# Norm sums as columns that share a PSUM bank, half of proj_a's sums accumulated in DRAM, and modulation spread wider, in a one-core decoder layer

## The chip, the cores and the metric

The kernel runs on one core of one Trainium2 chip. Its time is the device time of one execution in microseconds (us). The engines are TensorE (PE; PEld is its weight load), VectorE (DVE), ScalarE (ACT), GpSimd (POOL) and SyncE (SP), the last of which here only issues DMAs. POOL issues DMAs too, among them the ones that accumulate into DRAM, and ACT issues a few.

## The reference

One decoder layer on 1024 tokens of width 1024 in float32, followed by a final RMS norm. The parts that matter here:

```
u = modulate(rms_norm(x, norm1_g), sh1, sc1)
x = x + 0.5 * g1 * swiglu(u, ffn1_w_up, ffn1_w_down)
u = modulate(rms_norm(x, norm2_g), sh2, sc2)
z = u @ w_in + b_in
...
m = sigmoid(mg_a) * (ya @ proj_a) + sigmoid(mg_b) * (yb @ proj_b)
x = x + g2 * (m @ w_out)
u = modulate(rms_norm(x, norm3_g), sh3, sc3)
x = x + 0.5 * g3 * swiglu(u, ffn2_w_up, ffn2_w_down)
return rms_norm(x, final_g)
```

The nine shifts, scales and gates (sh1 to g3) come from one product of silu(c) with a 1024 x 9216 matrix (`mod_w`). `ya` is the output of a gated linear recurrence, `yb` that of an S5 state-space part.

## The kernel before

Data lie transposed: the 128 partitions hold features, the free dimension holds tokens. The 1024 features are eight tiles d = 0 to 7, and the tokens two halves h of 512. Float32 products are made from rounded parts: an operand is split into hi (rounded to fp32r by ACT) and lo (the rest, a subtraction on DVE), and a product is three passes, hi x hi, hi x lo and lo x hi. Many products are made in pairs by seven block products for what would be eight, with sums and differences of the operands and of the results on DVE (`pair`, `pair_operands`).

Nothing is issued as it is written. `Plan` records each instruction (line 437 issues them all, so most rows of the trace name that line) and `order` (line 257) simulates the engines with the costs of `cost` (line 205), and takes on each engine the earliest-written instruction that is ready and has buffers; `ahead` moves the rank of some forward. The result is a fixed order per engine, in which each engine later waits in turn. So a changed cost or a changed place in the text can move instructions far away.

Side work is spread through the products: `spread` (line 465) takes a job and a rate, and each block product calls `tick`, which lets the job go on by that rate. In the first feed-forward block, `background` (line 1723) runs `s5_setup` at rate 1.0 and 24 `modulations` at `MOD_RATE`; 24 more run later at `LATE_RATE`. A modulation (line 681) is a 512 KB weight load, one 128x1024 multiply with a running sum on DVE, and two one-column instructions. `finish_jobs` (line 478) puts what is left of the jobs into the program in one go.

An RMS norm needs the sum of x squared over features, which lie on partitions. `norm` (line 1670), at the start, squares on ACT and multiplies by a 128x128 matrix of ones in full float32 (two recorded passes per product), so that the bank holds the sum in all 128 rows of 512 columns. `square` and `rstd` (lines 704, 717), for the later norms, first add the squares on DVE, split the total into hi and lo, and make two fp32r products with the ones. Both then call `rstd_of` (line 729): a square root on ACT and a reciprocal on DVE over 128x512. ACT loads a table when it changes its function. `modulate` (line 738) multiplies x by the result, applies scale and shift on ACT, and splits hi and lo. The last norm, in `on_out` (line 1749), runs in pieces of 512, 256 and 256 tokens; its products with `final_g` run on DVE or, for tiles named in `OUT_POOL`, on POOL, each followed by its output DMA.

In `Mixer.run` (line 1495) `q_d` in DRAM holds the gated `proj_b` products. Four pairs of `proj_a` tiles follow. For each of their 16 results (tile d, half h), DVE multiplies the result by the gate loaded from `mga_d`, and adds what it loads from `q_d`. For the first two pairs (`M_OUT = 2`) the sum t is stored to `m_d` and loaded again, to free its buffer; for the last two it stays. Then each m is split into hi and lo, and the `w_out` products begin.

Of the kernel before, what the change touches and what calls it, by code (L numbers as in the profile page):

```python
# [10 lines left out]
F32 = mybir.dt.float32  # L11
# [34 lines left out]

SETUP_RATE, MOD_RATE, GAIN_RATE, LATE_RATE = 1.0, 0.18, 0.1, 0.2

# [25 lines left out]
class Plan:  # L74
# [130 lines left out]
    def cost(self, call, table):  # L205
# [236 lines left out]
class Layer:  # L442
# [260 lines left out]

    def square(self, st, x, d):

        nc = self.nc
        n = x.shape[1]
        sq = self.act()[:, :n]
        nc.scalar.activation(sq, x, AF.Square)
        if st[0] is None:  # L710
            st[0] = sq
        else:
            acc = self.act()[:, :n]
            nc.two(ALU.add, acc, st[0], sq)
            st[0] = acc

    def rstd(self, st):

        nc = self.nc
        n = st[0].shape[1]  # L720
        hi, lo = self.tmp(F32R)[:, :n], self.tmp(F32R)[:, :n]
        nc.scalar.activation(hi, st[0], AF.Copy)
        nc.vector.tensor_sub(lo, st[0], hi.bitcast(F32))
        ps = self.bank()[:, :n]
        self.mm(ps, self.ones, hi, True, False)
        self.mm(ps, self.ones, lo, False, True)
        return self.rstd_of(ps)

    def rstd_of(self, ps):
        nc = self.nc  # L730
        n = ps.shape[1]
        root = self.tmp()[:, :n]
        nc.scalar.activation(root, ps, AF.Sqrt, bias=self.eps, scale=1.0 / D)
        r = self.act()[:, :n]
        nc.vector.reciprocal(r, root)
        return r

    def modulate(self, x, r, l, d):

        nc = self.nc  # L740
        if r is not None:
            nc.two(ALU.mult, x, x, r)
# [274 lines left out]
def s5_setup(L):  # L1017
# [4 lines left out]
    L.decay = L.con("decay", [P, 16])  # L1022
    L.ident = L.con("ident", [P, P])
    st = {}

    def params():
        softplus_scales(L)
        yield
        make_identity(L.tc.nc, L.ident)
        bc = [L.act(), L.act()]  # L1030
# [216 lines left out]
class Mixer:  # L1247
# [247 lines left out]
    def run(self):  # L1495
# [54 lines left out]
        for p, pair in enumerate(PROJ_A):  # L1550
            c11, c12, c21, c22 = L.pair(L.pair_weights([io["proj_a"][d] for d in pair]), ya)
            for e, h, c in ((0, 0, c11), (1, 1, c22), (1, 0, c21), (0, 1, c12)):
                d = pair[e]
                t, r = self.load(self.mga_d, d, h), self.load(self.q_d, d, h)
                nc.vector.tensor_mul(t, t, c)
                nc.two(ALU.add, t, t, r)
                if p < M_OUT:
                    nc.sync.dma_start(self.m_d[d][:, h * H : (h + 1) * H], t)
                    with nc.ahead(GATED_AHEAD):
                        m[h][d] = self.load(self.m_d, d, h)  # L1560
                else:
                    m[h][d] = t
        ms = [[None] * 8, [None] * 8]
# [3 lines left out]
        x = [[None] * 8, [None] * 8]  # L1567
        st = [[None], [None]]
        u3 = L.u3 = [[], []]

        def put(d, h, ps):
# [3 lines left out]
            nc.sync.dma_start(L.x2_d[d][:, h * H : (h + 1) * H], t)  # L1575
            L.square(st[h], t, d)
            x[h][d] = self.load(L.x2_d, d, h) if d < W_PAIRED else t
            if d == ND - 1:
                s = L.rstd(st[h])
                for e in range(ND):  # L1580
# [40 lines left out]
def hybrid_layer(ctx: ExitStack, tc: tile.TileContext, io):  # L1621
# [5 lines left out]
    L.gsc = L.con("gsc", [P, 24])  # L1627
    L.ones = L.con("ones", [P, P], F32R)
    L.eps = L.con("eps", [P, 1])
    L.cact = L.con("cact", [P, D])  # L1630
    nc.vector.memset(L.eps, EPS)
    nc.vector.memset(L.ones.bitcast(F32), 1.0)

# [36 lines left out]
    def norm(h):  # L1670
        ps = L.bank()
        for d in range(ND):
            sq = L.act()
            nc.scalar.activation(sq, x[h][d], AF.Square)
            L.mm(ps, L.ones.bitcast(F32), sq, d == 0, d == ND - 1)
        r = L.rstd_of(ps)
        for d in range(ND):
            nc.two(ALU.mult, x[h][d], x[h][d], r)

# [46 lines left out]

    st = [[None], [None]]
    u2 = [[], []]

    def on_x(d, h, x):  # L1730
        L.square(st[h], x[h][d], d)
        if d == ND - 1:
            r = L.rstd(st[h])
            for e in range(ND):
# [11 lines left out]
    pieces = [(0, slice(0, H))] + [(1, slice(i * H // LAST, (i + 1) * H // LAST)) for i in range(LAST)]  # L1746
    st3 = [[None] for _ in pieces]

    def on_out(d, p, x):
        h, c = pieces[p]  # L1750
        L.square(st3[p], x[h][d][:, c], d)
        if d == ND - 1:
            scaled = {}
            for e in OUT_POOL[p]:
                scaled[e] = L.act()[:, : c.stop - c.start]
                nc.scalar.activation(scaled[e], x[h][e][:, c], AF.Copy, scale=L.col("final_g", e))
            r = L.rstd(st3[p])
            for e in range(ND):
                if e in scaled:
                    o = scaled[e]  # L1760
                    nc.gpsimd.tensor_mul(o, o, r)
                else:
# [108 lines left out]
```

## Time and profile before

| | us |
|---|---|
| median of 3 runs (2054.18 to 2054.97) | 2054.34 |
| the profiled execution | 2057.46 |
| its span in the trace | 2055.7 |
| PE busy in it | 1991.2 |
| DVE busy | 1554.1 |
| ACT busy | 1065.2 |
| POOL busy | 324.3 |

The mean granted TensorE clock is 0.987 of full speed. The profiled execution is 3.1 us above the median, and 1.8 us of its time lie outside the span. PE is busy for 97% of the span, so the whole rest is some 64 us: what matters is where those lie, and what PE waited for there.

### The profile page before, as it was taken

To read this page: it belongs to the slowest core of one execution; us is meant where nothing else is said; L and a number is where in the kernel's file an instruction comes from. 1 tells how busy PE (TensorE), PEld (TensorE's weight loads), DVE (VectorE), ACT (ScalarE), POOL (GpSimd) and SP (SyncE) were. 2 spreads that over 40 slices of the span, in tenths; PEclk is the share of its full clock that TensorE was granted. 3 is DMA by queue.
4 is the path that set the end of the run, shared out by engine and by line. 5 is a ranking of instruction groups with operands and counts; after the bars stand their busy time and mean duration, and the time that the engine had idled before them with its cause. 6 is when DMAs were issued, how large, how long until landed. Compare 5 with 4: busy or idle time off the path is not lost. (4 is left out here: it accounts for less than half of the span.)

```text
span 2055.7 us, 27034 instructions
## 1 busy us (share of the span) xinstructions
PE 1991.2 (97%) x8866; PEld 1635.7 (80%) x8866; DVE 1554.1 (76%) x3064; ACT 1065.2 (52%) x1842; POOL 324.3 (16%) x409
## 2 busy tenths in 40 slices
PE   6999999998999999999999999899999999999997
PEld 3888888886888878788878888677888888887886
DVE  8997777778969787767999597879544444497757
ACT  5744344344434574455789643447443344366753
POOL 0222122121011001100000011100111121134442
PEclk9999999999999999999999999999999999999998
DMA  7767676778756367787555689662765565589993
GB/s 261 192 156 208 180 197 185 198 193 265 238 156 178 130 172 206 217 251 248 174 173 196 230 253 280 210 235 74 173 159 133 129 150 136 123 210 220 203 230 127
DMA packets 188045, 393.06 MB, mean 191 GB/s; under 512 B 20992, under 2 KB 44672, under 8 KB 187904
## 3 DMA queue, kind: packets, MB, share of 16 engines
q1 hardware_dynamic: 121504, 278.45, 40.8%
q0 software_dynamic: 49536, 84.96, 24.6%
q10 hardware_dynamic: 16864, 27.93, 3.7%
q8 instruction: 69, 1.13, 0.2%
q14 instruction: 72, 0.59, 0.1%
HBM read 262.81 MB, written 92.27 MB: 173 GB/s over the span
## 5 line engine op out<-in xcount | busy, mean ns | idle before, releaser
L437 PE MATMUL ps_in<-act_in,wh_in 128*128 128x512 f32 (+1 forms) x5592 | 1685.6, 390 | 37.3 <-ACT act_in L437 12.5
L437 PEld LDWEIGHTS ps_in<-act_in,wh_in 128*128 128x128 f32 x5592 | 1050.0, 189 | 263.5 <-DVE act_in L437 17.2
L437 PE MATMUL ps_in<-act_in,wl_in 128*128 128x512 f32 (+1 forms) x2796 | 1047.7, 389 | 0.0
L437 ACT ACTIVATE wh_in<-wr_in 128x512 fp32r<-128x512 f32 (+2 forms) x544 | 323.8, 601 | 571.6 <-PE ps_in L437 451.7
L437 PEld LDWEIGHTS ps_in<-act_in,wl_in 128*128 128x128 f32 x2796 | 528.6, 189 | 107.6
L437 DVE TENSOR_TENSOR wl_in<-wr_in,wh_in 128x512 fp32r<-128x512 f32 (+2 forms) x544 | 352.3, 653 | 174.3 <-ACT wh_in L437 173.1
L437 DVE TENSOR_TENSOR act_in<-act_in,act_in 128x512 f32<-128x512 f32 (+3 forms) x632 | 400.0, 677 | 30.9 <-ACT act_in L437 24.0
L437 DVE TENSOR_TENSOR tmp_in<-ps_in,tmp_in 128x512 f32<-128x512 f32 x296 | 203.9, 689 | 160.3 <-PE ps_in L437 157.0
L437 ACT ACTIVATE act_in<-act_in 128x512 fp32r<-128x512 f32 (+3 forms) x414 | 238.0, 612 | 129.6 <-DVE act_in L437 107.0
L437 POOL DMA_DIRECT2D wr_in<-wr_in x148 | 136.5, 922 | 544.9 <-ACT wr_in L437 169.8
L437 ACT ACTIVATE tmp_in<-ps_in 128x512 f32<-128x512 f32 x130 | 76.3, 589 | 51.9 <-PE ps_in L437 44.2
L437 POOL DMA_DIRECT2D re_in<-in_ffn_w_up x40 | 35.6, 890 | 426.0 <-ACT re_in L437 307.0
L437 ACT ACTIVATE wr_in<-wr_in 128x512 f32<-128x512 f32 (+1 forms) x148 | 85.2, 594 | 23.3 <-DVE wl_in L437 21.9
L437 DVE TENSOR_TENSOR tmp_in<-tmp_in,ps_in 128x512 f32<-128x512 f32 x82 | 56.0, 685 | 41.7 <-PE ps_in L437 41.1
L437 ACT ACTIVATE wh_in<-re_in 128x512 fp32r<-128x512 f32 (+1 forms) x74 | 44.3, 599 | 67.9 <-PE ps_in L437 65.2
L437 DVE SCALAR_TENSOR_TENSOR mw_in<-mw_in,cact 128x1024 f32<-128x1024 f32 x56 | 68.3, 1220 | 8.3 <-DMA mw_in<-in_mod_w 8.2
L437 DVE TENSOR_TENSOR tmp_in<-tmp_in,tmp_in 128x512 f32<-128x512 f32 (+1 forms) x96 | 66.0, 688 | 5.8 <-ACT tmp_in L437 5.2
L437 DVE SCALAR_TENSOR_TENSOR act_in<-ps_in,mods,act_in 128x512 f32<-128x512 f32 (+1 forms) x68 | 46.2, 686 | 29.1 <-PE ps_in L437 28.9
L437 PE MATMUL ps_in<-act_in,act_in 128*128 128x256 f32 (+1 forms) x336 | 57.8, 317 | 3.8 <-DVE act_in L437 2.3
L437 PEld LDWEIGHTS ps_in<-act_in,act_in 128*128 128x128 f32 x336 | 49.2, 190 | 12.5 <-DVE act_in L437 4.9
L437 POOL DMA_DIRECT2D x_d<-tmp_in x48 | 50.2, 1266 | 53.0 <-ACT tmp_in L437 51.5
L437 ACT ACT_TABLE_LOAD x42 | 53.9, 1283 | 2.4 <-PEq L1860 1.7
(109 smaller groups left out, 1019.4 us busy)
## 6 DMA issues: line engine op xcount, KB each, us to landing
wr_in<-in_ffn_w_up SPq DMA_DIRECT2D x84, 512.0 KB, 3.7
mw_in<-in_mod_w SPq DMA_DIRECT2D x56, 512.0 KB, 4.3
wr_in<-wr_in POOLq DMA_DIRECT2D x108, 256.0 KB, 5.1
g_d<-tmp_in SPq DMA_DIRECT2D x88, 256.0 KB, 4.0
act_in<-g_d SPq DMA_DIRECT2D x88, 256.0 KB, 6.0
wr_in<-in_ffn_w_down SPq DMA_DIRECT2D x48, 384.0 KB, 4.0
wr_in<-in_w_in SPq DMA_DIRECT2D x36, 512.0 KB, 3.9
x_d<-tmp_in POOLq DMA_DIRECT2D x48, 256.0 KB, 7.5
```

What stands on the lines that cost most here:

```text
L437: getattr(getattr(self.nc, engine), method)(*map(self.place, args), **{k: self.place(v) for k, v in kwargs.items()})
```

## The change

Five things change.

1. `norm` copies the bank of sums to SBUF, and for each block of 128 tokens multiplies it by two columns of the identity, which puts the sums of 128 tokens into the rows of two columns: eight columns for 512 tokens. The square root and the reciprocal run on those (`rstd`), and one float32 product per block with the identity spreads the result back over 128 partitions, into a PSUM bank from which the multiplications read it.
2. The last norm does so too, without the copy: `square` splits the sum of the first seven squares and multiplies each block by two columns of ones; the four blocks share one bank, and only the first product opens it. The last square is added by a float32 product per block. POOL cannot read PSUM, so its tiles get a copy made by ACT.
3. The two norms between (`rstd_rows`) keep their form, but every norm now also takes a two-column square root right after its first square.
4. `proj_a`'s first two pairs no longer load `q_d`, add and store `m_d`: POOL adds t to `q_d` by an accumulating DMA, and SP loads `q_d` afterwards.
5. `MOD_RATE` falls from 0.18 to 0.14 and `LATE_RATE` from 0.2 to 0.16; `cost` gives small products on PE a higher floor.

```diff
-SETUP_RATE, MOD_RATE, GAIN_RATE, LATE_RATE = 1.0, 0.18, 0.1, 0.2
+SETUP_RATE, MOD_RATE, GAIN_RATE, LATE_RATE = 1.0, 0.14, 0.1, 0.16
...
-            return max(60.0, n * 1.7 if rhs.dtype == F32 else (n + 32) / 2.4), table
+            if rhs.dtype == F32:
+                return max(60.0 if method == "transpose" else 224.0, n * 1.7), table
+            return max(112.0 if n == 2 else 60.0, (n + 32) / 2.4), table
...
-    def square(self, st, x, d):
+    def square(self, st, x, d, rows=False):
         nc = self.nc
         n = x.shape[1]
         sq = self.act()[:, :n]
         nc.scalar.activation(sq, x, AF.Square)
-        if st[0] is None:
-            st[0] = sq
-        else:
+        if d == 0:
+            st[:] = [sq, None]
+            self.root(self.con(self.name("early"), [P, 2]), sq[:, :2])
+            return
+        if rows or d < ND - 1:
             acc = self.act()[:, :n]
             nc.two(ALU.add, acc, st[0], sq)
             st[0] = acc
-    def rstd(self, st):
+        if rows:
+            return
+        if d == ND - 2:
+            hi, lo = self.tmp(F32R)[:, :n], self.tmp(F32R)[:, :n]
+            nc.scalar.activation(hi, acc, AF.Copy)
+            nc.vector.tensor_sub(lo, acc, hi.bitcast(F32))
+            st[1] = self.bank()
+            for b in range(n // P):
+                c = slice(b * P, (b + 1) * P)
+                out = st[1][:, 2 * b : 2 * b + 2]
+                self.mm(out, hi[:, c], self.ones, b == 0, False, b > 0)
+                self.mm(out, lo[:, c], self.ones, False, True, b > 0)
+        if d == ND - 1:
+            for b in range(n // P):
+                self.mm(
+                    st[1][:, 2 * b : 2 * b + 2], sq[:, b * P : (b + 1) * P],
+                    self.ones.bitcast(F32), False, True, True,
+                )
+
+    def root(self, out, sums):
+        self.nc.scalar.activation(out, sums, AF.Sqrt, bias=self.eps, scale=1.0 / D)
...
+    def rstd(self, ps, n):
         nc = self.nc
+        k = n // P
+        r = self.con(self.name("rstd"), [P, 2 * k])
+        self.root(r, ps[:, : 2 * k])
+        nc.vector.reciprocal(r, r)
+        out = self.bank()[:, :n]
+        for b in range(k):
+            self.mm(
+                out[:, b * P : (b + 1) * P], r[:, 2 * b : 2 * b + 1].to_broadcast([P, P]),
+                self.ident, True, True,
+            )
+        return out
...
-                t, r = self.load(self.mga_d, d, h), self.load(self.q_d, d, h)
+                t = self.load(self.mga_d, d, h)
                 nc.vector.tensor_mul(t, t, c)
-                nc.two(ALU.add, t, t, r)
                 if p < M_OUT:
-                    nc.sync.dma_start(self.m_d[d][:, h * H : (h + 1) * H], t)
+                    nc.plus(self.q_d[d][:, h * H : (h + 1) * H], t)
                     with nc.ahead(GATED_AHEAD):
-                        m[h][d] = self.load(self.m_d, d, h)
+                        m[h][d] = self.load(self.q_d, d, h)
                 else:
+                    r = self.load(self.q_d, d, h)
+                    nc.two(ALU.add, t, t, r)
                     m[h][d] = t
...
-        r = L.rstd_of(ps)
+        sums = L.tmp()
+        nc.scalar.activation(sums, ps, AF.Copy)
+        ps = L.bank()
+        for b in range(H // P):
+            L.mm(
+                ps[:, 2 * b : 2 * b + 2], sums[:, b * P : (b + 1) * P], L.ident[:, :2],
+                True, True,
+            )
+        r = L.rstd(ps, H)
...
-            r = L.rstd(st3[p])
+            r = L.rstd(st3[p][1], c.stop - c.start)
+            if scaled:
+                r_copy = L.act()[:, : c.stop - c.start]
+                nc.scalar.activation(r_copy, r, AF.Copy)
             for e in range(ND):
                 if e in scaled:
                     o = scaled[e]
-                    nc.gpsimd.tensor_mul(o, o, r)
+                    nc.gpsimd.tensor_mul(o, o, r_copy)
```

Three places where the order of instructions moves, each before and after.

ACT, late in the first feed-forward block's up products (wh and act tiles are hi parts of weights and of operands; wr and re are raw weights). Before:

```order
L437 ACTIVATE wh_1007_in<-wr_995_in 128x384
L437 ACTIVATE wh_1025_in<-wr_1022_in 128x384
L437 ACTIVATE wh_1009_in<-wr_994_in 128x384
L437 ACTIVATE act_954_in<-act_909_in 128x512
L437 ACTIVATE act_956_in<-act_910_in 128x512
L437 ACTIVATE act_958_in<-act_911_in 128x512
L437 ACTIVATE wh_1027_in<-wr_1022_in 128x384
```

With the change (the weight part wh_1009<-wr_994 of before is wh_1013<-wr_998 here, and the operand parts act_954, act_956, act_958 are act_958, act_960, act_962):

```order
L439 ACTIVATE wh_1009_in<-re_1000_in 128x384
L439 ACTIVATE wh_1011_in<-wr_999_in 128x384
L439 ACTIVATE act_958_in<-act_913_in 128x512
L439 ACTIVATE wh_1005_in<-wr_998_in 128x384
L439 ACTIVATE act_960_in<-act_914_in 128x512
L439 ACTIVATE act_962_in<-act_915_in 128x512
L439 ACTIVATE wh_1029_in<-wr_1026_in 128x384
L439 ACTIVATE wh_1031_in<-wr_1026_in 128x384
L439 ACTIVATE tmp_1019_in<-ps_1015_in 128x512
L439 ACTIVATE wr_1026_in<-wr_1027_in 128x384
L439 ACTIVATE wh_1035_in<-wr_1027_in 128x384
L439 ACTIVATE wh_1013_in<-wr_998_in 128x384
```

The three operand parts stood behind that weight part; now it stands six rows behind the last of them.

SP, in `proj_a` (act tiles loaded from `mga_d` and `q_d`; the third and the fourth pair are act_2620 and later). Before:

```order
L437 DMA act_2620_in<-mga_d 128x512
L437 DMA act_2621_in<-q_d 128x512
L437 DMA act_2622_in<-mga_d 128x512
L437 DMA act_2623_in<-q_d 128x512
L437 DMA act_2624_in<-mga_d 128x512
L437 DMA act_2625_in<-q_d 128x512
L437 DMA act_2626_in<-mga_d 128x512
L437 DMA act_2627_in<-q_d 128x512
L437 DMA act_2652_in<-mga_d 128x512
L437 DMA act_2653_in<-q_d 128x512
L437 DMA act_2654_in<-mga_d 128x512
L437 DMA m_d<-act_2593_in 128x512
```

With the change:

```order
L439 DMA mw_3206_in<-in_mod_w 128x1024
L439 DMA wr_2768_in<-in_w_out 128x1024
L439 DMA act_2591_in<-q_d 128x512
L439 DMA act_2593_in<-q_d 128x512
L439 DMA act_2618_in<-mga_d 128x512
L439 DMA act_2619_in<-q_d 128x512
L439 DMA act_2620_in<-mga_d 128x512
L439 DMA act_2621_in<-q_d 128x512
L439 DMA act_2622_in<-mga_d 128x512
L439 DMA act_2623_in<-q_d 128x512
L439 DMA act_2624_in<-mga_d 128x512
L439 DMA act_2625_in<-q_d 128x512
```

The last store to `m_d` stood behind eleven loads of the last two pairs, and its load back stood twelve rows further; now the last two loads of accumulated sums (act_2591 and act_2593 of this piece) stand ahead of all of those loads.

DVE, the last instructions of the program. Before:

```order
L437 TENSOR_TENSOR tmp_4152_in<-act_4147_in,tmp_4151_in 128x256
L437 RECIPROCAL act_4155_in<-tmp_4154_in 128x256
L437 SCALAR_TENSOR_TENSOR act_4156_in<-act_4014_in,cols,act_4155_in 128x256
L437 SCALAR_TENSOR_TENSOR act_4157_in<-act_4018_in,cols,act_4155_in 128x256
L437 SCALAR_TENSOR_TENSOR act_4158_in<-act_4020_in,cols,act_4155_in 128x256
L437 SCALAR_TENSOR_TENSOR act_4159_in<-act_4024_in,cols,act_4155_in 128x256
L437 SCALAR_TENSOR_TENSOR act_4160_in<-act_4026_in,cols,act_4155_in 128x256
```

With the change:

```order
L439 TENSOR_TENSOR tmp_4148_in<-act_4146_in,tmp_4147_in 128x256
L439 RECIPROCAL rstd_4155<-rstd_4155 128x4
L439 SCALAR_TENSOR_TENSOR act_4158_in<-act_4014_in,cols,ps_4156_in 128x256
L439 SCALAR_TENSOR_TENSOR act_4159_in<-act_4018_in,cols,ps_4156_in 128x256
L439 SCALAR_TENSOR_TENSOR act_4160_in<-act_4020_in,cols,ps_4156_in 128x256
L439 SCALAR_TENSOR_TENSOR act_4161_in<-act_4024_in,cols,ps_4156_in 128x256
L439 SCALAR_TENSOR_TENSOR act_4162_in<-act_4026_in,cols,ps_4156_in 128x256
```

The reciprocal is on four columns, and the last products read it from a PSUM bank (ps_4156).

## Rows read from the trace of the kernel before

**Rows 1.** head of the page and its section 1, busy time by engine

```profile
span 2055.7 us, 27034 instructions
...
PE 1991.2 (97%) x8866; PEld 1635.7 (80%) x8866; DVE 1554.1 (76%) x3064; ACT 1065.2 (52%) x1842; POOL 324.3 (16%) x409
```

**Rows 2.** windows: length, busy us (instructions) by engine, granted clock, DMA share, GB/s

```profile
8.00:50.00 42.00, 32.42 (x90) 18.25 (x90) 41.90 (x153) 25.51 (x50) 0.00 (x0) 0.92 0.77 271
481.00:511.00 30.00, 21.55 (x82) 16.43 (x81) 24.68 (x55) 8.85 (x18) 5.38 (x7) 0.83 0.97 292
525.00:550.00 25.00, 24.48 (x108) 19.84 (x108) 23.88 (x49) 12.46 (x25) 0.63 (x1) 1.00 0.91 322
1294.00:1316.00 22.00, 14.88 (x51) 10.63 (x51) 19.74 (x37) 8.14 (x14) 2.62 (x3) 0.84 0.58 169
1380.00:1397.00 17.00, 14.09 (x55) 11.00 (x54) 14.80 (x21) 13.03 (x21) 0.00 (x0) 0.90 0.45 150
2041.00:2055.00 14.00, 1.39 (x4) 0.59 (x3) 9.46 (x14) 2.12 (x5) 8.69 (x11) 0.58 0.43 150
```

**Rows 3.** timeline of DVE, start: start us, us, instruction, count, idle before and releaser

```profile
18.86 3.35 DVE L437 RECIPROCAL act_in<-tmp_in 128x512 f32<-128x512 f32 x1
```

**Rows 4.** timeline of PE, 481 to 511 us

```profile
493.09 0.50 PE L437 MATMUL ps_in<-act_in,wh_in 128*128 128x512 f32 x1 [3.16 <-ACT act_in L437]
...
498.62 0.98 PE L437 MATMUL ps_in<-cb_in,act_in 128*128 128x32 f32 x8
503.10 1.22 PE L437 MATMUL ps_in<-act_in,wh_in 128*128 128x512 f32 x2 [3.50 <-DVE tmp_in L437]
```

**Rows 5.** timeline of ACT, then of DVE, 481 to 511 us

```profile
491.99 0.52 ACT L437 ACTIVATE wh_in<-wr_in 128x384 fp32r<-128x384 f32 x1 [5.81 <-DMA wr_in<-wr_in]
...
502.36 0.68 DVE L437 TENSOR_TENSOR tmp_in<-ps_in,tmp_in 128x512 f32<-128x512 f32 x1
```

**Rows 6.** timeline of PE, 1294 to 1316 us

```profile
1309.59 1.91 PE L437 MATMUL ps_in<-act_in,wh_in 128*128 128x512 f32 x4
...
1313.86 1.07 PE L437 MATMUL ps_in<-act_in,wh_in 128*128 128x512 f32 x4
```

**Rows 7.** timelines of SP and DVE, and section 6 of the page

```profile
1275.47 0.33 SPq L437 DMA_DIRECT2D act_in<-mga_d  x1
...
1285.56 0.32 SPq L437 DMA_DIRECT2D m_d<-act_in  x1
...
1295.28 0.32 SPq L437 DMA_DIRECT2D act_in<-m_d  x1
...
1281.59 0.68 DVE L437 TENSOR_TENSOR act_in<-act_in,ps_in 128x512 f32<-128x512 f32 x1
...
x_d<-tmp_in POOLq DMA_DIRECT2D x48, 256.0 KB, 7.5
```

**Rows 8.** timelines of ACT, DVE and PE, third norm

```profile
1380.35 1.28 ACT L437 ACT_TABLE_LOAD   x1
1381.64 0.69 ACT L437 ACTIVATE tmp_in<-ps_in,eps 128x512 f32<-128x512 f32 x1
...
1382.94 0.76 DVE L437 SCALAR_TENSOR_TENSOR act_in<-ps_in,mods,act_in 128x512 f32<-128x512 f32 x1 [1.81 <-PE ps_in L437]
1383.61 3.35 DVE L437 RECIPROCAL act_in<-tmp_in 128x512 f32<-128x512 f32 x1
...
1390.83 0.49 PE L437 MATMUL ps_in<-act_in,wh_in 128*128 128x512 f32 x1 [2.47 <-ACT act_in L437]
```

**Rows 9.** timeline of PE, then of DVE, end of the program

```profile
2044.89 0.58 PE L437 MATMUL ps_in<-tmp_in,ones 128*128 128x256 f32 x1 [3.67 <-ACT tmp_in L437]
...
2041.58 0.48 DVE L437 SCALAR_TENSOR_TENSOR act_in<-ps_in,mods,act_in 128x256 f32<-128x256 f32 x1
...
2047.08 1.75 DVE L437 RECIPROCAL act_in<-tmp_in 128x256 f32<-128x256 f32 x1 [1.24 <-ACT tmp_in L437]
2048.87 3.56 DVE L437 SCALAR_TENSOR_TENSOR act_in<-act_in,cols,act_in 128x256 f32<-128x256 f32 x5
```

More of the change, by code (lines that the diff above doesn't have):

```diff
@@ L719, in rstd, with rstd_rows @@
+        if d == ND - 1:
[6 more added lines that the diff above has]
+        self.nc.scalar.activation(out, sums, AF.Sqrt, bias=self.eps, scale=1.0 / D)
+    def rstd_rows(self, st):
         nc = self.nc
-        n = st[0].shape[1]
-        hi, lo = self.tmp(F32R)[:, :n], self.tmp(F32R)[:, :n]
+        hi, lo = self.tmp(F32R), self.tmp(F32R)
@@ L722, in rstd @@
         nc.scalar.activation(hi, st[0], AF.Copy)
         nc.vector.tensor_sub(lo, st[0], hi.bitcast(F32))
[L724 to L734, printed above, removed]
+        ps = self.bank()
@@ L735, in rstd_of @@
+        self.mm(ps, self.ones_p, hi, True, False)
+        self.mm(ps, self.ones_p, lo, False, True)
+        root = self.tmp()
+        self.root(root, ps)
+        r = self.act()
         nc.vector.reciprocal(r, root)
         return r
+    def rstd(self, ps, n):
+        nc = self.nc
+        k = n // P
[9 more added lines that the diff above has]
+        return out
@@ L741, in modulate @@
         if r is not None:
-            nc.two(ALU.mult, x, x, r)
+            nc.vector.tensor_mul(x, x, r)
         hi, lo = self.act(F32R), self.act(F32R)
@@ L1028, in params @@
         yield
-        make_identity(L.tc.nc, L.ident)
         bc = [L.act(), L.act()]
@@ L1567, in run @@
         x = [[None] * 8, [None] * 8]
-        st = [[None], [None]]
+        st = [[], []]
         u3 = L.u3 = [[], []]
@@ L1575, in put @@
             nc.sync.dma_start(L.x2_d[d][:, h * H : (h + 1) * H], t)
-            L.square(st[h], t, d)
+            L.square(st[h], t, d, True)
             x[h][d] = self.load(L.x2_d, d, h) if d < W_PAIRED else t
             if d == ND - 1:
-                s = L.rstd(st[h])
+                s = L.rstd_rows(st[h])
                 for e in range(ND):
@@ L1627, in hybrid_layer @@
     L.gsc = L.con("gsc", [P, 24])
-    L.ones = L.con("ones", [P, P], F32R)
+    L.ones_p = L.con("ones_p", [P, P], F32R)
+    ones = L.ones_p.bitcast(F32)
+    L.ones = L.ones_p[:, :2]
+    L.ident = L.con("ident", [P, P])
+    make_identity(tc.nc, L.ident)
     L.eps = L.con("eps", [P, 1])
@@ L1631, in hybrid_layer @@
     nc.vector.memset(L.eps, EPS)
-    nc.vector.memset(L.ones.bitcast(F32), 1.0)
+    nc.vector.memset(ones, 1.0)
     nc.scalar.dma_start(L.cact, io["c"].partition_broadcast(P))
@@ L1674, in norm @@
             nc.scalar.activation(sq, x[h][d], AF.Square)
-            L.mm(ps, L.ones.bitcast(F32), sq, d == 0, d == ND - 1)
-        r = L.rstd_of(ps)
+            L.mm(ps, ones, sq, d == 0, d == ND - 1)
+        sums = L.tmp()
[7 more added lines that the diff above has]
+        r = L.rstd(ps, H)
         for d in range(ND):
-            nc.two(ALU.mult, x[h][d], x[h][d], r)
+            nc.vector.tensor_mul(x[h][d], x[h][d], r)
     def step(h, k):
@@ L1725, in background @@
         L.spread(modulations([(i, d) for i in (2, 4, 3) for d in range(8)]), MOD_RATE)
-    st = [[None], [None]]
+    st = [[], []]
     u2 = [[], []]
     def on_x(d, h, x):
-        L.square(st[h], x[h][d], d)
+        L.square(st[h], x[h][d], d, True)
         if d == ND - 1:
-            r = L.rstd(st[h])
+            r = L.rstd_rows(st[h])
             for e in range(ND):
@@ L1746, in hybrid_layer @@
     pieces = [(0, slice(0, H))] + [(1, slice(i * H // LAST, (i + 1) * H // LAST)) for i in range(LAST)]
-    st3 = [[None] for _ in pieces]
+    st3 = [[] for _ in pieces]
     def on_out(d, p, x):
```

1 line of the change is left out of this document (removed).

## The prediction

> **What bounds the kernel now.** I read the head of the page first: PE is busy for 1991.2 of 2055.7 us [rows 1], so no change off PE's path can save more than the 64.5 us in which it stands still, and what it loses at a lowered clock. Then the windows say where those lie [rows 2]. PE stands still for 42.00 - 32.42 = 9.6 us in the start, where DVE is busy for 41.90 of 42 us; for 8.45 us between 481 and 511; for 7.1 us between 1294 and 1316; for 2.9 us around the third norm; and after 2041 there is only the tail. These are the places that the change can help. Last I read, in each, the chain that ends the wait.
>
> A stall also costs after it has ended. At 1309.59 four passes of 128x512 take 1.91 us, at 1313.86 four take 1.07 [rows 6]: the granted clock is at its lower level (1.2 GHz) behind the stalls and rises to 2.4 GHz. The mean granted clock gives the bound: 0.83 over 30 us means 0.17 x 2 x 30 = 10.2 us at half speed, some of it idle anyway. The loss is thus at most 5.1 us, and at least (10.2 - 8.45) / 2 = 0.9; I take the middle, 3. Likewise 0 to 3.5 in 1294 to 1316 (taken: 2) and 0.2 to 1.7 around the third norm (taken: 1.2) [rows 2]. With these the three stretches hold 11.5, 9.1 and 4.1 us that could come back.
>
> **The change, part by part.**
>
> Start: +1 (-2 to +3). Two reciprocals of 3.35 us [rows 3] become reciprocals of eight columns. From 3.35 at 512 columns and 1.75 at 256 [rows 3, 9] one costs 0.15 us and 6.25 ns a column, so 0.2 each: DVE saves 6.3 us. But DVE paces the start [rows 2], and the new order puts other DVE work ahead of the third product group: six weight parts of 256 columns, some twenty small setup instructions and a modulation, about 5 us by the share that such work takes there. What is left, 1.3 us, goes against a longer chain: a copy, a table load, then 4 + 4 float32 products, twice. Before, the table load lay in the wait for the sums; now it stands behind the copy, 1.28 us [rows 8]. The small products cost 0.98 / 8 = 0.12 us a pass [rows 4]; 16 passes are 2.0 us a half, partly beside the first product group, which needs only the first half. I set 2.3 us of waits against the 1.3; the low end is no wait, the high end all of it in line.
>
> On that table load: the square root at 1381.64 starts where the load of 1380.35 ends [rows 8], so the row gives 1.28 us and nothing behind it. The Trainium skill, "ScalarE: Activation LUTs", section "What ACT_TABLE_LOAD costs", adds a drain of about 1.38 us to every switch, 2.66 in all; by it the start would be 1.4 us dearer and the result 2041. The row speaks against it, and I give it one chance in ten, inside the forecast.
>
> Setup and modulations: -9 (-11.5 to -3), and +1 (0 to +2) behind it. The 3.16 us stall at 493.09 waits for operand parts on ACT [rows 4]. ACT had stood for 5.81 us until 491.99, for a weight that a DMA was still summing [rows 5], and those parts were queued behind it. In the new order they come first, so the DMA's lateness no longer reaches them. The 3.50 us stall at 503.10 waits for a sum on DVE that starts at 502.36 [rows 4, 5]; some 5 us of s5 instructions stood ahead of it there, and the last s5 products were PE's at 498.62. With fewer modulations per product the s5 setup now ends before these: its last products on PE stand 223 rows earlier. Both stalls and the clock behind them, 3.16 + 3.50 + 3 = 9.7, I expect gone but for 0.7; the three smaller ones (1.8) I leave. The small end is that one of the two stays, and the clock with it. What is late next: six modulations that `finish_jobs` now puts in at once, and others moved into 505 to 560, where DVE is busy for 23.88 of 25 us [rows 2] and PE already loses 0.5. One more such hit is the +1.
>
> `proj_a`: -4 (-9 to +2.5). Eight additions of 0.68 us [rows 7] leave DVE, but they lie before 1277, where it has gaps, and are worth nothing themselves. What counts is the last m tile. Its store to `m_d` stood at 1285.56 on SP and its load back at 1295.28 [rows 7], into the stretch in which PE waits 7.1 us for split operands [rows 2]. Now the load stands ahead of the last two pairs' loads and lands about ten us sooner, so its parts come when DVE and PE reach them. The price is SP's order: these loads wait for an accumulation that POOL issues once DVE has made its product; by my count of DVE's order that is near 1270.5, some 11 us ahead of 1281.59. The nearest row for its landing is POOL's accumulation into `x_d`, 7.5 us [rows 7], so 1278, and all loads behind it start 2.5 us later than 1275.47. The first is needed at 1281.59 [rows 7]. Before, some 6 to 8 us lay between such an issue and its use; so DVE waits 2 to 3 us in a stretch where it is full. Gain 9.1, less 2.5 of that wait, less about 2.5 that I expect of stalls from DVE's own load: -4. The ends: the wait never shows, or the load saves nothing and the wait is all paid.
>
> By the Trainium skill, "DMA: Bandwidth & Descriptors", section "Anatomy of one DMA", a POOL transfer takes 2.0 us and its bytes over 436 GB/s, 2.6 us for 256 KB; then nothing would wait, the term would be -6.5 and the result 2037. The row of 7.5 us, from this kernel's own accumulations, speaks against it; one in ten again, inside the forecast.
>
> Third norm: -3.5 (-4.1 to 0). The reciprocal started at 1383.61, behind an instruction that had waited 1.81 us for PE at 1382.94, though the square root was out at 1382.33 [rows 8]. In the new order that instruction stands behind it, which is 1.2 us; two weight parts, 0.6 each, also leave the way to the first operand. That is 2.4 of the 2.9 us that PE waits, most of the clock's 1.2 goes too. The early square root costs ACT nothing where it idles. The second norm has no stall and gives nothing.
>
> End: 0 (-4 to +2). After the last product, at 2044.89 - 3.67 = 2041.2 [rows 9], 14.5 us pass to the end of the span. Off this: the reciprocal of 1.75 falls to 0.2, the last five products on DVE from 0.71 us each [rows 9], two SBUF operands beside POOL, to 0.48, as the one with a PSUM operand at 2041.58 takes; and the reciprocal of the piece before no longer delays DVE. 1.6 + 1.15 + 1.6 = 4.3, less 0.5 for the broadcast. But the new products come into PE's full stream: 24 passes for the first piece, 12 for the second, at 0.12 [rows 4] 4.3 us, less 0.7 for the wide ones removed. -3.8 + 3.6 is nothing within what I can tell. The low end has the small products wait in gaps, the high end has each chain pay the broadcast in line.
>
> Elsewhere the order is the same but for neighbours: nothing.
>
> **Sum.** +1 - 9 + 1 - 4 - 3.5 + 0 = -14.5. The profiled execution is 3.1 us above the median of the runs; its own 2057.46 would become 2043, the median 2054.34 becomes 2039.8, **say 2040**.
>
> **Rivals.**
>
> Gains come back elsewhere. The changed costs shuffle the order everywhere, and DVE is at 95% just behind 511 [rows 2]; a sum that is late by 3 us there makes a new stall with its clock, 4 to 6 us each. Two such stalls leave 8 to 12 less of the 14.5: 2048 to 2052. For it: the windows with the long stalls, 481 to 511 and 1294 to 1316, are ones in which DVE is busy for 82 and 90% [rows 2]. Against: PE loses only 0.5 us at 95% between 525 and 550.
>
> The accumulations land late: slower. The eight go through POOL's one queue, between weight sums that POOL waits for, and SP stands at each load until its sum has landed; behind it stand the gate, `q_d` and `w_out` loads of the whole next stage. Every us that the last landing moves past 1278 is one us for DVE, which has no slack between 1281 and 1309, and for PE. It turns the sign when the -14.5 are eaten, at a landing past 1292.5: two more landings of 7.5 us in line ahead of the last one, instead of side by side. Three in line, 22.5 us late, give +8, and the clock behind such a wait up to 2 more: 2062 to 2064. Against: the DMA engines took POOL's other transfers side by side, and 7.5 is already a landing among others.
>
> The change doesn't do what it says: the copies and products of the start and the end eat their reciprocals and the order at 481 to 511 keeps another wait: 2046 to 2054, with the first rival.
>
> **How the numbers follow.** My forecast's own cases get 0.66: 2031 to 2047, that is 2040 less 2.5 and 5 (the low ends of setup and `proj_a`) and 1.5 of the small terms, and more by 6 or 6.5 (the high end of one of the two). Gains that come back get 0.16, the change that does not do what it says 0.08 (2046 to 2054), late accumulations 0.10. For 8 in 10 I take 2029 to 2053, up to which the first two rivals reach. About 0.2% (4 us) is what a measurement of this kernel can tell from no change, so faster means below 2050.2: 0.66 and some 0.14 of the 0.24 make 0.80; same 0.09; slower 0.11.
>
> **What would show it.** No stall over 1 us on PE near 480 to 500 (times shift by up to 12 us), the s5 products some 60 us earlier, idle under 4 us where it was 7.1, under 1 us at the third norm, last product to end near 10.5 us. I am wrong if SP waits more than 4 us for an accumulation, if new stalls of 3 us stand behind 505, or if the start's third product group begins over 3 us later.

## The result and the profile after

The changed kernel takes 2030.05 us (median of 4 runs, 2028.92 to 2031.69), the kernel before 2054.26 beside it: ratio 0.9882, interval 0.9865 to 0.9900, so 24.2 us faster. The forecast was 2040, 14.5 less. The profiled execution of the changed kernel took 2030.39 us, that of before 2057.46: the traces differ by 27, since before's execution lay 3.1 above its median.

Where the time went can be read place by place, because both kernels have the same 8,388 passes with split weight parts on PE, in the same sequence but for a few that swap places with near ones. I took the start of each in both traces; the table gives how their median difference moves from one quiet stretch to the next. It compares one trace with one trace.

| place (us in the trace of before) | moved, us | forecast |
|---|---|---|
| start, to 60 | +3.65 | +1 |
| setup and modulations, 60 to 560 | -13.69 | -9 + 1 |
| 560 to 1240 | -6.05 (+1.90 near 765, -3.77 near 868, -4.18 from 950 to 1110) | 0 |
| `proj_a`, 1260 to 1355 | -5.59 | -4 |
| third norm, 1375 to 1470 | -3.09 | -3.5 |
| second feed-forward block, near 1883 | -1.37 | 0 |
| end | -0.90 | 0 |
| sum | -27.0 | -14.5 |

The head of the page of the changed kernel:

```profile
span 2028.6 us, 27165 instructions
...
PE 1988.1 (98%) x8940; PEld 1639.1 (81%) x8940; DVE 1537.1 (76%) x3053; ACT 1068.3 (53%) x1853; POOL 330.3 (16%) x417
```

Its windows, to be laid beside [rows 2]; those behind the start are moved by 10 to 25 us, as the places are. 932 to 1015 and 1215 to 1258 are new here; the first answers to 945 to 1030 of before:

```profile
8.00:50.00 42.00, 32.83 (x106) 20.15 (x107) 41.54 (x184) 26.28 (x52) 0.00 (x0) 0.88 0.84 284
470.00:500.00 30.00, 30.00 (x134) 24.79 (x133) 30.00 (x54) 19.51 (x40) 6.10 (x8) 1.00 0.91 289
515.00:540.00 25.00, 25.00 (x112) 20.71 (x111) 24.49 (x47) 12.70 (x24) 0.00 (x0) 1.00 0.93 315
932.00:1015.00 83.00, 82.95 (x402) 69.96 (x402) 75.04 (x136) 63.33 (x96) 0.41 (x4) 1.00 0.56 180
1215.00:1258.00 43.00, 43.00 (x192) 35.60 (x191) 26.66 (x50) 13.00 (x22) 12.28 (x14) 1.00 0.91 223
1278.00:1300.00 22.00, 19.36 (x78) 14.96 (x77) 20.52 (x37) 9.04 (x16) 2.65 (x3) 0.92 0.53 136
1359.00:1376.00 17.00, 16.58 (x72) 13.16 (x71) 15.39 (x22) 12.79 (x21) 1.03 (x2) 1.00 0.36 123
2018.60:2028.60 10.00, 1.92 (x13) 1.56 (x12) 3.20 (x9) 1.88 (x5) 2.09 (x3) 0.68 0.32 105
```

Where PE stood still for 8.45 of 30 us it now has no gap at full clock, though DVE is busy for all of the 30. Of the windows shown, the granted clock is below 1.00 in the start, in `proj_a` and in the tail. PE's timeline of the changed kernel, stalls, the last s5 products and the last narrow products of the second norm:

```profile
35.04 0.50 PE L439 MATMUL ps_in<-ident,tmp_in 128*128 128x2 f32 x4
...
36.80 1.13 PE L439 MATMUL ps_in<-ident,rstd 128*128 128x128 f32 x8 [1.26 <-DVE mods L439]
40.78 0.80 PE L439 MATMUL ps_in<-act_in,wh_in 128*128 128x512 f32 x1 [2.85 <-ACT act_in L439]
43.50 0.79 PE L439 MATMUL ps_in<-act_in,wh_in 128*128 128x512 f32 x1 [1.92 <-DVE act_in L439]
...
443.31 0.98 PE L439 MATMUL ps_in<-cb_in,act_in 128*128 128x32 f32 x8
...
755.37 0.49 PE L439 MATMUL ps_in<-act_in,wh_in 128*128 128x512 f32 x1 [4.15 <-ACT act_in L439]
...
858.22 0.73 PE L439 MATMUL ps_in<-act_in,wh_in 128*128 128x512 f32 x2 [0.97 <-DVE tmp_in L439]
...
1282.92 0.50 PE L439 MATMUL ps_in<-act_in,wh_in 128*128 128x512 f32 x1 [1.65 <-DVE act_in L439]
1285.33 0.80 PE L439 MATMUL ps_in<-act_in,wh_in 128*128 128x512 f32 x1 [0.98 <-DVE act_in L439]
...
1367.56 0.50 PE L439 MATMUL ps_in<-act_in,wh_in 128*128 128x512 f32 x1 [0.40 <-DVE act_in L439]
...
1869.72 0.73 PE L439 MATMUL ps_in<-act_in,wh_in 128*128 128x512 f32 x2 [1.83 <-DVE tmp_in L439]
...
2018.35 0.28 PE L439 MATMUL ps_in<-act_in,wl_in 128*128 128x256 f32 x1
```

The s5 products end at 443.31, 55 us sooner than in [rows 4], and PE has no gap from 470 to 500 and from 515 to 540. The 7.1 us of [rows 2] in `proj_a` have shrunk to two stalls of 1.65 and 0.98, the 2.47 us of [rows 8] to 0.40. From the end of the last product, 2018.63, to the end of the span pass 9.97 us instead of 14.5. Behind the start, the longest stall left is the 4.15 us at 755.37; its counterpart in the trace of before, 3.73 us at 764.75, is in none of the windows of [rows 2]. The loss is in the start. DVE's timeline there and at the two later norms, with a line of before first:

```profile
33.42 5.51 DVE L437 TENSOR_TENSOR act_in<-act_in,act_in 128x512 f32<-128x512 f32 x9
```

```profile
35.31 1.22 DVE L439 SCALAR_TENSOR_TENSOR wr_in<-wr_in,cact 128x1024 f32<-128x1024 f32 x1
...
36.45 0.20 DVE L439 RECIPROCAL rstd<-rstd 128x8 f32<-128x8 f32 x1
...
37.97 4.87 DVE L439 TENSOR_TENSOR act_in<-act_in,ps_in 128x512 f32<-128x512 f32 x8
...
1360.60 3.35 DVE L439 RECIPROCAL act_in<-tmp_in 128x512 f32<-128x512 f32 x1 [1.14 <-ACT tmp_in L439]
...
2022.83 1.66 DVE L439 SCALAR_TENSOR_TENSOR act_in<-act_in,cols,ps_in 128x256 f32<-128x256 f32 x4 [0.45 <-ACT act_in L439]
```

The second norm's reciprocal costs 0.2 us, but it starts at 36.45. Its sums are late: of the eight narrow passes that turn them into columns, the last four stand on PE behind the second product group, at 35.04, and ACT waits 2.05 us for them. The root is out at 35.85; the modulation of 35.31 then holds the reciprocal for 0.6 us more. The multiplications begin at 37.97, when the broadcast of 36.80 has ended; in the trace of before they begin at 33.42. At the third norm no instruction from PSUM stands ahead of the reciprocal any more.

ACT's timeline, the first norm and the second:

```profile
17.45 1.28 ACT L439 ACT_TABLE_LOAD   x1
18.74 0.27 ACT L439 ACTIVATE rstd<-ps_in,eps 128x8 f32<-128x8 f32 x1
...
35.58 0.27 ACT L439 ACTIVATE rstd<-ps_in,eps 128x8 f32<-128x8 f32 x1 [2.05 <-PE ps_in L439]
```

The first square root starts 0.01 us behind the load's end, as in [rows 8]. The drain of 1.38 us that the Trainium skill, "ScalarE: Activation LUTs", section "What ACT_TABLE_LOAD costs", adds to a switch does not show here either.

SP's waits for the accumulations (us in total, times, longest), between 1205 and 1245, then between 1245 and 1275:

```profile
SPq L439 <- DMA q_d<-act_in: 15.5, 5, 7.1
```

```profile
SPq L439 <- DMA q_d<-act_in: 0.2, 1, 0.2
```

So SP does wait for the accumulations, once for 7.1 us; but for the last two, which stand ahead of the loads of the last two pairs, it waits 0.2. They land 6.2 us after their issue by the median of eight (256 KB each, 3.7 to 10.1). The estimate of 2.6 us that follows from the Trainium skill, "DMA: Bandwidth & Descriptors", section "Anatomy of one DMA", is not seen. The long waits cost nothing here: PE has no gap from 1215 to 1258.

### The profile page after: what moved, and what is told of

Read it like the earlier page. It is cut to its first block, busy times and chain, and to the rows that moved or that the text cites. A ratio compares the mean times of both kernels' runs of the same rounds, so it can differ in the third digit from the quotient of the medians.

```text
span 2028.6 us, 27165 instructions
## 1 busy us (share of the span) xinstructions
PE 1988.1 (98%) x8940; PEld 1639.1 (81%) x8940; DVE 1537.1 (76%) x3053; ACT 1068.3 (53%) x1853; POOL 330.3 (16%) x417
## 4 chain that ended last, share of the span: by engine, by line
PE 61%; DVE 7%; ACT 5%; DMA 4%; issue 3%; POOL 0%; ACTq 0%; POOLq 0%; SPq 0%; DVEq 0%
PE ps_in L439 61%; DVE act_in L439 4%; ACT act_in L439 3%; DVE tmp_in L439 1%; DMA act_in<-g_d 1%; ACT tmp_in L439 1%; DVE wl_in L439 1%; DMA wr_in<-wr_in 1%; ACT wh_in L439 1%; DMA x_d<-tmp_in 0%; DMA act_in<-mga_d 0%; POOL act_in L439 0%; DMA act_in<-q_d 0%; DMA mga_d<-tmp_in 0%; ACT L439 0%
## 5 line engine op out<-in xcount | busy, mean ns | idle before, releaser
L439 PEld LDWEIGHTS ps_in<-act_in,wh_in 128*128 128x128 f32 x5592 | 1046.0, 188 | 239.9 <-DVE act_in L439 10.3
L439 DVE TENSOR_TENSOR act_in<-act_in,act_in 128x512 fp32r<-128x512 f32 (+3 forms) x605 | 383.8, 676 | 27.0 <-ACT act_in L439 23.4
L439 ACT ACTIVATE wr_in<-wr_in 128x512 f32<-128x512 f32 (+1 forms) x148 | 84.9, 593 | 15.7 <-DVE wl_in L439 14.4
```

The lines of the kernel that those rows point to most:

```text
L439: getattr(getattr(self.nc, engine), method)(*map(self.place, args), **{k: self.place(v) for k, v in kwargs.items()})
```

## The experiments

Three of them put one part of the change into the kernel before; five take one part out of the changed kernel or alter it; the last two repeat. "Moved" is read as in the table above.

### The modulation rate alone

```diff
-SETUP_RATE, MOD_RATE, GAIN_RATE, LATE_RATE = 1.0, 0.18, 0.1, 0.2
+SETUP_RATE, MOD_RATE, GAIN_RATE, LATE_RATE = 1.0, 0.14, 0.1, 0.2
```

> The kernel before with MOD_RATE 0.14 alone. Between the spans the two profiles differ by 13.7 us from 450 to 545 (8.45 + 0.5 us of stalls and some 4.5 us of lowered clock). Theory A (each part acts where its own stall lies, this one through the order of the s5 setup and the modulations): 2054.3 - 13 = 2041 (2039 to 2044), no stall over 1 us between 470 and 545, and the two stalls at 764 and 868 stay as they are. Rival B (the whole order is reshuffled by any edit; the gain belongs to no single part): 2047 to 2056, with new stalls of 2 us or more elsewhere before 560. Rival C (the new start, by its lighter DVE, is what frees the s5 setup): 2050 to 2055 with the stalls at 493 and 503 still there.

Measured: 2045.98 us, ratio 0.9958 (0.9943 to 0.9972), 2 us above the range of theory A. Between 60 and 560 the products moved by -10.31, so the rate alone takes both long stalls away; near 868 by another -3.21; and between 950 and 1110 by +3.51. A window, and PE's timeline of this kernel:

```profile
470.00:500.00 30.00, 28.77 (x117) 20.75 (x116) 29.18 (x54) 17.38 (x37) 4.46 (x6) 1.00 0.98 298
```

```profile
951.61 0.51 PE L437 MATMUL ps_in<-act_in,act_in 128*128 128x512 f32 x1 [0.97 <-ACT act_in L437]
...
971.78 0.38 PE L437 MATMUL ps_in<-act_in,act_in 128*128 128x256 f32 x1 [1.45 <-ACT act_in L437]
```

The products of the recurrence wait for parts here, 0.97 and 1.45 us, in a stretch in which DVE of the kernel before is busy for 96% (the window of the next experiment). I read it so that DVE paces the stretch, and that what PE brings into it as a lead is lost there.

### The late rate alone

```diff
-SETUP_RATE, MOD_RATE, GAIN_RATE, LATE_RATE = 1.0, 0.18, 0.1, 0.2
+SETUP_RATE, MOD_RATE, GAIN_RATE, LATE_RATE = 1.0, 0.18, 0.1, 0.16
```

> The kernel before with LATE_RATE 0.16 alone. In the changed kernel PE gains 3.8 us near 868 and 4.1 us from 950 to 1100, where I had forecast nothing, and loses 1.9 us near 755. Theory A: the modulations taken out of this stretch are the cause: 2054.3 - 7 = 2047 (2045 to 2050), DVE busy below 92% from 950 to 1030 and the stall at 868 under 1.5 us. Rival B (these belong to the reshuffling that the rest of the change brings): 2052 to 2056, the stalls at 868 and from 950 on as before.

Measured: 2050.42 us (10 runs), ratio 0.9977 (0.9967 to 0.9986). Of the 6.7 us that its trace is shorter, 4.21 lie between 950 and 1110. The stall near 868 was expected under 1.5 us and is still 2.54 long (2.69 before), so the gain near 868 in the table is not the late rate's. The window 945 to 1030, first of the kernel before, then of this one:

```profile
945.00:1030.00 85.00, 82.40 (x394) 68.31 (x393) 81.42 (x146) 62.82 (x94) 0.59 (x6) 1.00 0.56 185
```

```profile
945.00:1030.00 85.00, 85.00 (x415) 71.97 (x415) 76.80 (x141) 65.19 (x98) 0.41 (x4) 1.00 0.56 183
```

With fewer modulations in it DVE falls from 96 to 90% and PE has no gap. So the late rate has a gain of its own. That it also takes away the limit that eats the other parts' gains fits the traces, but the changed kernel with the old `LATE_RATE` was not run.

### The sums in DRAM alone

```diff
...
-t, r = self.load(self.mga_d, d, h), self.load(self.q_d, d, h)
+t = self.load(self.mga_d, d, h)
...
-    nc.sync.dma_start(self.m_d[d][:, h * H : (h + 1) * H], t)
+    nc.plus(self.q_d[d][:, h * H : (h + 1) * H], t)
...
```

> The kernel before with the accumulation into q_d alone, in place of load, addition, store and load. Theory A: PE's stalls between 1294 and 1316 fall from 7.1 us to 3 or less and the clock comes back: 2054.3 - 5.6 = 2048.7 (2047 to 2051). Rival (SP waits for the accumulations and the loads behind are late): SP's first load from mga_d behind them is over 4 us late, stalls of 5 us or more remain, 2052 to 2058. A landing of the accumulations near 7.5 us is what the forecast took; near 2.6 the skill's fit would be right.

Measured: 2050.31 us (10 runs), ratio 0.9985 (0.9974 to 0.9997). `proj_a` moved by -5.04 of the full change's -5.59. PE's and SP's timelines of this kernel:

```profile
1299.05 0.50 PE L437 MATMUL ps_in<-act_in,wh_in 128*128 128x512 f32 x1 [1.65 <-DVE act_in L437]
...
1301.45 0.50 PE L437 MATMUL ps_in<-act_in,wh_in 128*128 128x512 f32 x1 [0.99 <-DVE act_in L437]
```

```profile
1274.28 0.46 SPq L437 DMA_DIRECT2D act_in<-mga_d  x1
```

The two stalls that are left are those of the changed kernel. The first load of the last two pairs is issued at 1274.28, 1.2 us sooner than in [rows 7] and not 2.5 later. Here too 4.41 us near 868 came before 2.93 given back between 950 and 1110. The median is 4.6 us lower, a little less than `proj_a` alone.

### The changed kernel with the old norm at the start

```diff
-        sums = L.tmp()
-        nc.scalar.activation(sums, ps, AF.Copy)
...
-        r = L.rstd(ps, H)
+        root = L.tmp()
+        L.root(root, ps)
+        r = L.act()
+        nc.vector.reciprocal(r, root)
```

> The changed kernel with the first two norms as they were (square root and reciprocal over 512 columns). By the offsets of PE's instructions the new start costs 3.6 us. Theory A: this comes back: 2030.0 - 3.6 = 2026.4 (2025 to 2028), with the first stall-free stretch starting near 49 us instead of 52, all else alike. Rival B (the lighter start moves the side work, which pays elsewhere): 2030 to 2036, with stalls behind 60 us that the changed kernel has not.

Measured: 2026.54 us, ratio 0.9862 (0.9847 to 0.9877). Its interval overlaps the changed kernel's 0.9865 to 0.9900; what tells is the trace. The start moved by -3.48 against the changed kernel, back to within 0.3 us of before: as it stands in the change, the new norm of the start is a loss.

### The changed kernel without the early square root

```diff
-            self.root(self.con(self.name("early"), [P, 2]), sq[:, :2])
```

> The changed kernel without the two-column square root after each norm's first square. In the changed kernel the third norm gains 3.1 us; its table load no longer stands right ahead of the square root, and the DVE instruction that stood ahead of the reciprocal stands behind it. Theory A (the order is the cause; before, the load ended within 0.1 us of the sums): the same time, 2029 to 2032, the third norm's PE stall stays under 1 us, and at most 1.3 us come back at the end, where the load would stand in the tail. Rival (the table is the cause): 2032 to 2034, a stall of 2 us or more at the third norm.

Measured: 2037.08 us, ratio 0.9897 (0.9863 to 0.9931), by which it is not separated from the changed kernel's 0.9882. In the trace the third norm moved by +3.33: the gain is gone there. Timelines of ACT, of DVE and of PE, then ACT's line of the changed kernel at the same place:

```profile
1366.04 1.28 ACT L439 ACT_TABLE_LOAD   x1
1367.34 0.69 ACT L439 ACTIVATE tmp_in<-ps_in,eps 128x512 f32<-128x512 f32 x1
```

```profile
1368.63 0.75 DVE L439 SCALAR_TENSOR_TENSOR act_in<-ps_in,mods,act_in 128x512 f32<-128x512 f32 x1 [1.80 <-PE ps_in L439]
1369.30 3.34 DVE L439 RECIPROCAL act_in<-tmp_in 128x512 f32<-128x512 f32 x1
```

```profile
1376.51 0.50 PE L439 MATMUL ps_in<-act_in,wh_in 128*128 128x512 f32 x1 [2.48 <-ACT act_in L439]
```

```profile
1359.88 0.69 ACT L439 ACTIVATE tmp_in<-ps_in,eps 128x512 f32<-128x512 f32 x1 [1.23 <-PE ps_in L439]
```

This is [rows 8] again, to 0.02 us: the load stands directly ahead of the square root, DVE's instruction that waits 1.80 us for PE stands ahead of the reciprocal, and PE waits 2.48. The load's own time is not what costs: in the changed kernel ACT waits 1.23 us for the sums at that place, and the load of 1.28 us fills just this wait. What differs is the order. `cost` counts 1285 ns for a table load; by my reading, without the early root it therefore takes the reciprocal for not ready and puts that instruction first. My expectation that the order stays without the early root fell.

### The changed kernel with the old last norm

```diff
...
-            r = L.rstd(st3[p][1], c.stop - c.start)
-            if scaled:
-                r_copy = L.act()[:, : c.stop - c.start]
-                nc.scalar.activation(r_copy, r, AF.Copy)
+            r = r_copy = L.rstd_rows(st3[p])
```

> The changed kernel with the last norm over 512 and 256 columns as before. From the last product's end to the end of the span it is 10.0 us in the changed kernel and was 14.5; against this, small products of some 3.6 us stand in PE's stream. Theory A: the sum of both, 0.9 us, comes back: 2030 to 2032. Rival (the small products cost nothing, since PE has gaps there): 4 us come back, 2033 to 2036.

Measured: 2032.93 us, ratio 0.9882 (0.9852 to 0.9911), the changed kernel's own ratio. The end moved by +0.64. PE's timeline:

```profile
2014.43 0.28 PE L439 MATMUL ps_in<-act_in,wl_in 128*128 128x256 f32 x1
2017.65 0.38 PE L439 MATMUL ps_in<-tmp_in,ones_p 128*128 128x256 f32 x1 [2.94 <-ACT tmp_in L439]
```

The last product ends at 2014.71 in a span of 2028.4, so the tail is 13.7 us instead of 9.97. The new form wins that 3.7, and pays 3.0 of it back: its last product stands 3.0 us later against the products near 1990, behind the small products in PE's full stream.

### The changed kernel with the old costs of small products

```diff
-            if rhs.dtype == F32:
-                return max(60.0 if method == "transpose" else 224.0, n * 1.7), table
-            return max(112.0 if n == 2 else 60.0, (n + 32) / 2.4), table
+            if rhs.dtype == F32:
+                return max(60.0, n * 1.7), table
+            return max(60.0, (n + 32) / 2.4), table
```

> The changed kernel with the planner's former costs of small products on PE. Theory A (the costs matter little): 2029 to 2033, the s5 setup's last products some 12 us later, no stall over 1 us between 450 and 545. Rival B (the result hangs on the order by chance): outside of 2026 to 2034, with a stall of over 2 us at a place where neither kernel has one.

Measured: 2034.66 us, ratio 0.9897 (0.9864 to 0.9930), not separated from the changed kernel's 0.9882. The trace moved by +4.32 between 350 and 560 and by -2.06 in the start. PE's timeline, the last s5 products and a stall:

```profile
454.44 0.98 PE L439 MATMUL ps_in<-cb_in,act_in 128*128 128x32 f32 x8
...
862.45 1.22 PE L439 MATMUL ps_in<-act_in,wh_in 128*128 128x512 f32 x2 [3.62 <-DVE tmp_in L439]
```

The last s5 products stand at 454.44, 11 us later than in the changed kernel (443.31), as expected. With `MOD_RATE` alone they stand at 451.70, so of the 55 us by which they end sooner the rate gives 47, and the higher floors some 8 to 11. That the floors also win some 4 us between 350 and 560 is one trace's word. The 2.06 in the start says little, since a repeat of the changed kernel differs there by 1.75.

### The second norm planned 40 us ahead

In the start of the changed kernel PE waits for the second norm; this moves the rank of the whole norm forward in the planner, its products on PE as well as its reciprocal.

```diff
-    norm(1)
+    with nc.ahead(40):
+        norm(1)
```

> The changed kernel with the second norm's rank moved forward by 40, so that its sums stand ahead of the first product group and its reciprocal ahead of two modulations on DVE. In the changed kernel the second reciprocal waits for two modulations (1.22 us each) and for its sums, which PE makes after the first group; by PE's offsets the start costs 3.6 us. Theory A (that place is the cause): 3 to 5 us come back, 2025 to 2028, with the second norm's multiplications starting near 34 instead of 38 us. Rival (DVE paces the start whatever stands first): 2029 to 2032.

Measured: 2025.24 us, ratio 0.9845 (0.9817 to 0.9874). The start moved by -6.92 against the changed kernel, more than expected.

### Both once more on one chip

> The changed kernel once more, beside the next run on the same chip. Theory A (the second norm, which stands behind two modulations in the start, costs about 4 us): 2028 to 2033 us, with the stalls of 2.85 and 1.92 us on PE near 41 and 44. Rival (the difference of the version with the second norm ahead was the chip's or the neighbours' luck): both kernels lie within 2 us of each other.

> The changed kernel with the second norm planned 40 us ahead, again, with more rounds. Theory A: 4 to 7 us below the changed kernel on this chip, 2023 to 2028 us, start at the same place as in its first run (one PE stall near 38 of about 2.2 us), everything behind 60 us as in the changed kernel within 2 us. Rival: within 2 us of the changed kernel, the start's gain given back behind it.

Measured: the changed kernel 2032.19 us (2028.12 to 2035.06; ratio 0.9894, 0.9877 to 0.9910), the version with the second norm ahead 2023.96 (2021.94 to 2026.27; ratio 0.9859, 0.9843 to 0.9875). Their runs do not overlap. The start moved by -6.15 against the first trace of the changed kernel, and by -7.9 against its repeat, whose start is 1.75 us longer than the first's. It is the best of the kernels here. Its window at the start, and the timelines of DVE and PE:

```profile
8.00:50.00 42.00, 37.44 (x134) 24.28 (x134) 41.73 (x184) 26.05 (x52) 0.00 (x0) 0.96 0.82 285
```

```profile
30.16 0.19 DVE L439 RECIPROCAL rstd<-rstd 128x8 f32<-128x8 f32 x1
...
32.53 4.87 DVE L439 TENSOR_TENSOR act_in<-act_in,ps_in 128x512 f32<-128x512 f32 x8
```

```profile
28.80 0.95 PE L439 MATMUL ps_in<-ident,tmp_in 128*128 128x2 f32 x8
...
38.05 0.69 PE L439 MATMUL ps_in<-act_in,wh_in 128*128 128x512 f32 x1 [2.21 <-DVE act_in L439]
```

DVE does as much as before, but all eight narrow passes now stand at 28.80, in the middle of the first product group, the reciprocal comes 6.3 us sooner, PE works for 37.4 instead of 32.8 us, and one stall of 2.21 replaces three. Against the kernel before, the start is now some 2.5 us shorter (3.65 - 6.15).

The repeat of the changed kernel shows what one trace is worth near 860. PE's timeline of that run, to be held against 858.22 above:

```profile
860.83 0.73 PE L439 MATMUL ps_in<-act_in,wh_in 128*128 128x512 f32 x2 [1.82 <-DVE tmp_in L439]
```

The same kernel waits 0.97 us here in one run and 1.82 in another. So does the stall of the second feed-forward block: 1.83 at 1869.72, 0.65 in the repeat.

## Why the prediction was right, and where it was not

The sign and the range hold, and but for the start the stretches read from [rows 2] with long waits are places in which the change won. But 2030.05 lies only 1 us inside the range and below 2031, the low end of the forecast's own cases: the sum came out 10 us short (12.5 between the two traces), from three terms too small and one too good. Without the unforeseen 4.2 us of the late rate the time would have been near 2034.

**"Elsewhere the order is the same but for neighbours: nothing"** is the step that failed: -7.4 us lie there (-6.05 and -1.37). -4.18 of it is the lower `LATE_RATE`, which alone gives -4.21 in the same place. I had read windows only where I looked for the change, and none of the stretch at 945 to 1030, where the stalls of before are short but DVE is busy for 96%; the stalls of 3.73, 2.69 and 2.65 us near 764, 868 and 1883 were left out too. The -3.77 near 868 and the -1.37 near 1883 are no settled gain: in these runs the stall near 868 was anything from 0 to 3.6 us, and differs between two runs of one kernel. In before's trace it was among the long ones, 2.69, which fits its 3.1 us above the median.

**Setup and modulations** (-9 + 1, came -13.7). The mechanism is as read: both stalls gone, s5 products 55 us sooner, `MOD_RATE` alone worth -10.3. Three sizes were off. The clock's share, of which I took the middle, 3, came out near its bound of 5.1: 13.7 less the window's 8.45 us of idle time, the smaller stalls of 1.8 among it, leaves 5.2. This is a difference and was not measured by itself. And the +1 of new stalls behind did not come, though DVE works without a pause: 515 to 540 shows no gap. `MOD_RATE` alone leaves 1.23 us of idle time between 470 and 500, and 3.4 of the 13.7 come from other parts. The old costs of small products lose 4.3 in this stretch, which points to the floors; by one trace it is not settled.

**`proj_a`** (-4, came -5.6, of it -5.0 by the sums in DRAM alone). The last sum comes back sooner, as forecast. The 2.5 us for late accumulations were wrong. The last one is issued near where I had counted it (1252.97, some 1269 in the times of before), but it lands after 5.0 us instead of 7.5, SP waits 0.2 us for it, and the loads behind come about 1 us sooner instead of 2.5 later. That SP has lost its `m_d` stores fits this, but was not tried by itself. The 2.5 us I expected of DVE's own load are what is left: 1.65 + 0.98.

**Third norm** (-3.5, came -3.1). The working was right: the waiting instruction stands behind the reciprocal. I had not seen why, and took the early root for a side matter; the experiment shows that the order hangs on it.

**Start** (+1, came +3.65, outside my range of -2 to +3). The order of DVE's work was charged to the third product group as a sum of durations. What decided was the second norm's chain: its last narrow passes stand behind the whole second product group, its multiplications begin 4.6 us later than before, and two stalls of 2.85 and 1.92 follow, with passes at the lower clock behind them. Modulations ahead of the reciprocal hold it for only 0.6 us of this. The +3.65 is one trace's; in the repeat of the changed kernel it is 5.4. The table load cost what its row said.

**End** (0, came -0.9). Both halves were about right: the tail shrank by 4.5 where I had 3.8, and the small products took most of it back, 3.0 by the experiment where I had 3.6. Four multiplications with a PSUM operand take 1.66 us, 0.41 each, less than the 0.48 I took.

**The rivals.** Gains did come back elsewhere, for parts alone: with `MOD_RATE` or the sums alone, 3.5 and 2.9 us are lost again between 950 and 1110, in a stretch where DVE is busy for 96%, which is near that rival's reason. It did not strike the whole change, which fits that this lowers `LATE_RATE`. Late accumulations occurred in part: SP waited 15.7 us for six of them, up to 7.1, more than the 4 us under which I said I would be wrong. But these waits lay ahead of 1245, where PE has no gap, so they cost nothing, and the condition was badly chosen: only the last landing, which the rival itself named, could hurt. Of the condition on the start, the third product group begins at 40.78 against 40.62, so it does not begin late; from its second pass on it is 2.6 to 4.6 us late.

## What to carry to other kernels

A stretch with few waits on the bounding engine can still be at its limit: read the second engine's busy share there (96% here), for it will eat the lead that other changes bring, and lightening it may be worth more with them than alone, which these traces suggest and no run here tests. When a scheduler orders the instructions, a modelled cost or a two-column dummy instruction can be worth more than its own time, by what it lets stand ahead; and a shortened instruction wins nothing if what it needs is planned late, as the second reciprocal shows: its sums stood behind a product group, which one line then repaired for 6 to 8 us of the start.

## What the runs showed of the hardware that was not expected

A table load of 1.28 us was followed by its square root within 0.02 us in the three places shown (17.45 here, 1366.04 without the early root, 1380.35 before). Accumulating transfers of 256 KB into `q_d` took 6.2 us to land by the median, 6.9 with the sums alone, and single ones 3.7 to 10.1. A square root of 8 columns took 0.27 us, a reciprocal of 8 columns 0.20. In the start, the pass behind the stall of 1.92 us took 0.79 us, where the one behind a stall of 1.65 us in `proj_a` took 0.50; the granted clock of the start's window fell to 0.88 from 0.92 before, so the two stalls there cost more than their idle time.
